# The second layer norm of an encoder layer: scale and shift on the turned tiles, GpSimd makes x2, tiles at multiples of 64 bytes

## The chip, the cores and the metric

The kernel runs on one core of a Trainium2 chip. The engines are named as the profile names them: PE is TensorE (matmuls and transposes), DVE VectorE, ACT ScalarE, POOL GpSimd, SP SyncE, whose queue issues most of the DMAs. The metric is the device time of one launch in microseconds (us), the median of the runs. On-chip memory is SBUF, with 128 partitions; matmul results land in PSUM.

## The reference

One layer of an encoder on a sequence of 1024 tokens, model width 1024, all in float32:

```python
x = layer_norm(DEEPNORM_ALPHA * x + 0.5 * swiglu_ffn(x, ffn1_w_gu[l], ffn1_w_down[l]), ln1_g[l], ln1_b[l])
x = layer_norm(DEEPNORM_ALPHA * x + hybrid_mixer(x, w_in[l], w_gla_a2[l], b_gla_a[l], gla_norm_g[l], w_out[l]),
               ln2_g[l], ln2_b[l])
x = layer_norm(DEEPNORM_ALPHA * x + 0.5 * swiglu_ffn(x, ffn2_w_gu[l], ffn2_w_down[l]), ln3_g[l], ln3_b[l])
```

The layer norm takes mean and variance over the 1024 features of a token and returns (x - mean) * rsqrt(var + 1e-5) * g + b. The feed-forward part is (silu(h @ w_g) * (h @ w_u)) @ w_down with an inner width of 2816. The mixer is one input projection, four heads of chunked gated linear attention, eight heads of sparse attention over selected keys, and one output projection, w_out. The case is about the line in the middle: the output projection, the second layer norm, and the first matrix products of the second feed-forward part, which read its result, x2. x2 is needed twice: as that part's input, and later, token by token, as the residual of the third layer norm.

## The kernel before, in words

Matrix products are done in three passes with a hi and a lo part: ACT rounds a float32 tile to its hi part (`Weights.split`, L96), DVE subtracts to get the lo part (L97), and PE sums hi by hi, lo by hi and hi by lo. Both operands are split so, weights and activations. The feed-forward products run on block sums of the matrices, a Strassen-like scheme with seven products instead of eight: of a quarter of the weights (tiles `rw`, sums made by POOL in L341 to L344, hi and lo parts `whiq` and `wloq`) and of the activations (quarters 11, 12, 21, 22 and their sums T1 to T4).

The tokens are eight blocks of 128. In the second layer norm's stage, at the end of `run`, the loop over the blocks b does the following for each:

- `proj_tok`: 24 matmuls give the second half (512 features) of the output projection in PSUM (`pt`). The first half was made before: of blocks 0 to 3 during the attention (L1645 stores it), of blocks 4 to 7 in a loop after it (tile `x1h`, L1669). The block's tile `acc[b]`, 128 tokens by 1024 features, was loaded with it; the profile calls it `x`.
- L1686, DVE: ALPHA times x plus the projection.
- `layer_norm` (L238 to L255): two `bn_stats` of 512 features, `bn_aggr`, variance plus epsilon (`ve`) on DVE; the reciprocal root `rs` by a power on POOL (L224, 128x1); `nb`, minus mean times rs, on DVE (L252); x * rs + nb on ACT, in place, 128x1024 (L253); times g on POOL (L254); plus b on DVE (L255). g and b are rows repeated in all partitions (`g_bc`, `b_bc`).
- L1688: 512 KB of x2 go to DRAM for the third norm's residual.
- From b = 2 on, `feed` turns block b - 2 in: `turn_in` makes, for each half, four PE transposes of 128x128 into one PSUM tile `tp` (two buffers, L282); ACT takes the hi part and DVE the lo part of it straight from PSUM, and ACT copies it back over the token-major half (L285, `keep`), because the sums T1 to T4 are made from turned halves later (L1270 to L1273: DVE, POOL, DVE, POOL; `split_turned` then splits them from SBUF). `b_h` and `b_l` are hi and lo parts of quarters 11 and 21; `xh` and `xl` those of the later quarters and sums.

Blocks 0 to 5 are turned inside the loop (4 and 5 as the last two); blocks 6 and 7 are turned in as fills between the matmuls of the first product of `gate_up`, together with the sums of block pairs (0,4), (1,5), (2,6), (3,7). That product is of quarters 11 and 21 with the gate weights; its two PSUM tiles are read by ACT's silu (L460), which loads its function table first, and are then used by the product after next.

The order: from the loop on, PE's instructions stand in the order in which the code makes them (`in_order`). The order on DVE, ACT, POOL and SP is set by a scheduler that plays the program through a timeline of its own when the kernel is built. At run time each engine takes its instructions strictly in the order so found and waits at each for what it needs. SBUF pools of the stage: `ln2` (`lp`, g, b and the `x1h` tiles), and `sums2` (`xp`).

Of the kernel before, what the change touches and what calls it, by code (L numbers as in the profile page):

```python
# [7 lines left out]
F32 = mybir.dt.float32  # L8
# [10 lines left out]
P = 128  # L19
# [96 lines left out]
class Block:  # L116
    def __init__(self, ctx, tc, aps):
# [9 lines left out]
        self.wpool = E(tc.tile_pool(name="wpool", bufs=1))  # L127
        self.ps_pj = E(tc.tile_pool(name="ps_pj", bufs=2, space=PSUM))
# [4 lines left out]
        nc.gpsimd.memset(self.neghalf, -0.5)  # L133
        self.w = Weights(tc, self.wpool)
# [5 lines left out]
        self.q_tiles = {}  # L140

# [88 lines left out]

    def layer_norm(self, t, g_bc, b_bc, scale=1.0, st=None):

        nc = self.nc
        made = st is not None
        if not made:
            st = self.small.tile([P, 2, 6], F32, tag="st", name=self.uid("st"))
            for c in range(2):
                nc.vector.bn_stats(st[:, c, :], t[:, c * 512 : (c + 1) * 512])  # L238
# [6 lines left out]
        if made:  # L245
            nc.vector.scalar_tensor_tensor(t, t, mv[:, 0:1], g_bc, ALU.subtract, ALU.mult)
            for c in range(2):
                cs = slice(c * 512, (c + 1) * 512)
                nc.vector.scalar_tensor_tensor(t[:, cs], t[:, cs], rs, b_bc[:, cs], ALU.mult, ALU.add)
        else:  # L250
            nb = self.small.tile([P, 1], F32, tag="nb", name=self.uid("nb"))
            nc.vector.scalar_tensor_tensor(nb, mv[:, 0:1], -1.0, rs, ALU.mult, ALU.mult)  # L252
            nc.scalar.activation(t, t, AF.Identity, bias=nb, scale=rs)  # L253
            nc.gpsimd.tensor_mul(t, t, g_bc)  # L254
            nc.vector.tensor_add(t, t, b_bc)  # L255
# [22 lines left out]
    def turn_in(self, src, j, name, keep=False):  # L278

        pt = self.ps_tp.tile([P, 4, P], F32, tag="tp", name=self.uid("tp"))  # L280
        for k in range(4):
            self.nc.tensor.transpose(pt[:, k, :], src[:, k * P : (k + 1) * P], self.ident)  # L282
# [13 lines left out]
    def feed(self, b, t):  # L296

        names = ("12", "22") if b >= NB // 2 else ("11", "21")
        for i, name in enumerate(names):
            self.turn_in(t[:, i * 512 : i * 512 + 512], b % 4, name, keep=True)  # L300
# [199 lines left out]
    def down(self, w_down, h_dram, t_dram, ps, load, after_block, after_all=None, ordered=None):  # L500
# [43 lines left out]
        def stat(b, c):  # L544
            if b not in stats:
# [1221 lines left out]
```

## Time and profile before

| | before |
|---|---|
| median of 3 runs | 1992.12 us (1988.24 to 1994.79) |
| profiled execution | 1986.98 us, its span 1985.2 us |
| granted PE clock, mean | 0.99 |
| busy: PE / DVE / ACT / POOL | 1932.2 / 1493.5 / 834.0 / 602.3 us |
| PE idle in the whole span | 53 us |
| stage of the change on the time axis | 1285 to 1365 us |
| PE waiting in that stage | 5.6 us, once |

A line of a timeline is: start, duration, engine, line of the kernel, operation, out<-in, shape, and in brackets how long the engine idled before it and what released it. A line of a chain of waits is: start, length, engine, tile and line. A line of the groups has the count, total busy time, mean duration in ns, and idle time with its releaser. Lines by tile have the shortest, the median and the longest duration in ns. A line of a table of stretches has the window, its length, busy time (and count) of PE, PE's weight loads, DVE, ACT and POOL, then granted clock, share of DMA time, GB/s.

### The profile page before, as it was taken

What the parts mean: (1) busy time and instruction counts of PE and PEld (TensorE: products, weight loads), DVE (VectorE), ACT (ScalarE), POOL (GpSimd) and SP (SyncE); (2) the same over time, 40 slices, a digit from 0 to 9 for tenths busy, and PEclk for the clock granted to TensorE, in tenths of its full rate; (3) what the DMA queues carried; (4) which work ended last, traced back from release to release, by engine and by line L of the source; (5) the groups of instructions that cost most, each with busy time, mean ns of one, the idle gap of its engine ahead of it and who ended that gap; (6) DMA issues with size and microseconds to landing.
All of it is one profiled execution on the core that took longest, in us unless ns stands there. A gap on an engine that the chain in (4) does not pass through costs nothing.

```text
span 1985.2 us, 26633 instructions
## 1 busy us (share of the span) xinstructions
PE 1932.2 (97%) x9576; PEld 1586.4 (80%) x9576; DVE 1493.5 (75%) x2333; ACT 834.0 (42%) x1340; POOL 602.3 (30%) x507
## 2 busy tenths in 40 slices
PE   9999999999999999999899899998999999999997
PEld 7788888888888788777687678787888888888886
DVE  8777887785677768899968567477778777857677
ACT  5333333334334345798553456354333233235331
POOL 4454454430001102144343000054444544510011
PEclk9999999999999999998999999999999999999999
DMA  5454454478656322022105741522444544587564
GB/s 180 146 185 152 155 182 146 149 254 305 200 175 202 99 85 85 22 65 62 45 33 170 186 106 39 201 97 95 159 138 147 187 148 149 178 290 251 193 199 151
DMA packets 193925, 298.43 MB, mean 150 GB/s; under 512 B 16496, under 2 KB 100608, under 8 KB 193792
## 3 DMA queue, kind: packets, MB, share of 16 engines
q1 hardware_dynamic: 189888, 291.48, 44.8%
q10 hardware_dynamic: 3264, 3.15, 0.5%
q0 software_dynamic: 640, 2.10, 0.3%
q8 instruction: 75, 1.23, 0.3%
q14 instruction: 58, 0.48, 0.1%
HBM read 205.96 MB, written 90.70 MB: 149 GB/s over the span
## 4 chain that ended last, share of the span: by engine, by line
PE 72%; DVE 13%; DMA 5%; issue 3%; ACT 3%; POOL 2%; SPq 0%; POOLq 0%; DVEq 0%; ACTq 0%
PE pd L536 18%; PE pq L362 11%; PE pq L363 11%; PE pq L364 11%; DVE junk L830 3%; PE pf L701 2%; PE pf L700 2%; PE pf L702 2%; PE pt L717 2%; PE pt L719 2%; PE pt L718 2%; PE pv L1186 2%; PE tpe L1170 2%; PE lg L1143 1%; DMA rd<-h_dram 1%
## 5 line engine op out<-in xcount | busy, mean ns | idle before, releaser
L97 DVE TENSOR_TENSOR wloq<-rw,whiq 128x512 fp32r<-128x512 f32 (+2 forms) x211 | 209.8, 996 | 130.3 <-ACT whiq L96 129.5
L97 DVE TENSOR_TENSOR wlod<-rd,whid 128x1024 fp32r<-128x1024 f32 x154 | 186.1, 1221 | 129.4 <-ACT whid L96 128.7
L96 ACT ACTIVATE whid<-rd 128x1024 fp32r<-128x1024 f32 x154 | 161.1, 1059 | 243.7 <-PE pd L536 167.5
L96 ACT ACTIVATE whiq<-rw 128x512 fp32r<-128x512 f32 (+2 forms) x211 | 164.2, 797 | 206.9 <-POOL rw L344 105.0
L536 PE MATMUL pd<-wlod,whid 128*128 128x512 f32 x616 | 239.8, 390 | 0.9 <-DVE wlod L97 0.8
L536 PE MATMUL pd<-whid,wlod 128*128 128x512 f32 x616 | 239.3, 389 | 0.0
L536 PE MATMUL pd<-whid 128*128 128x512 f32 x616 | 235.0, 391 | 0.7 <-ACT whid L96 0.7
L362 PE MATMUL pq<-b_h,whiq 128*128 128x512 f32 x576 | 226.1, 392 | 2.3 <-DVE c L411 1.3
L364 PE MATMUL pq<-b_h,wloq 128*128 128x512 f32 x576 | 224.9, 391 | 0.5 <-DVE wloq L97 0.5
L363 PE MATMUL pq<-b_l,whiq 128*128 128x512 f32 x576 | 225.0, 391 | 0.0
L224 POOL TENSOR_TENSOR rs<-ve,neghalf 128x1 f32<-128x1 f32 x24 | 35.4, 1476 | 540.5 <-DVE ve L242 540.5
L476 ACT ACTIVATE c<-c 128x512 f32<-128x512 f32 x80 | 50.7, 634 | 266.5 <-DVE c L398 169.7
L362 PE MATMUL pq<-xh,whiq 128*128 128x512 f32 x352 | 136.9, 389 | 0.0
L363 PE MATMUL pq<-xl,whiq 128*128 128x512 f32 x352 | 136.9, 389 | 0.0
L364 PE MATMUL pq<-xh,wloq 128*128 128x512 f32 x352 | 136.9, 389 | 0.0
L536 PEld LDWEIGHTS pd<-wlod,whid 128*128 128x128 f32 x616 | 115.7, 188 | 25.8 <-DVE wlod L97 2.1
L536 PEld LDWEIGHTS pd<-whid 128*128 128x128 f32 x616 | 115.5, 188 | 25.2 <-ACT whid L96 1.7
L536 PEld LDWEIGHTS pd<-whid,wlod 128*128 128x128 f32 x616 | 115.6, 188 | 24.1
L717 PE MATMUL pt<-whi,xh 128*128 128x512 f32 x320 | 131.3, 410 | 2.4 <-ACT stage L1531 1.6
L362 PEld LDWEIGHTS pq<-b_h,whiq 128*128 128x128 f32 x576 | 108.7, 189 | 25.8 <-ACT whiq L96 1.8
L364 PEld LDWEIGHTS pq<-b_h,wloq 128*128 128x128 f32 x576 | 108.6, 188 | 23.9 <-DVE wloq L97 1.1
L718 PE MATMUL pt<-wlo,xh 128*128 128x512 f32 x320 | 127.6, 399 | 0.0
(275 smaller groups left out, 4484.7 us busy)
## 6 DMA issues: line engine op xcount, KB each, us to landing
rw<-in_ffn_w_gu_dram SPq DMA_DIRECT2D x87, 512.0 KB, 4.3
rd<-h_dram SPq DMA_DIRECT2D x154, 256.0 KB, 3.5
h_dram<-c SPq DMA_DIRECT2D x148, 256.0 KB, 3.2
rt<-in_ffn_w_down_dram SPq DMA_DIRECT2D x44, 512.0 KB, 3.6
t_dram<-rt SPq DMA_DIRECT2D x44, 512.0 KB, 3.0
rd<-t_dram SPq DMA_DIRECT2D x88, 256.0 KB, 3.7
rd<-in_ffn_w_down_dram SPq DMA_DIRECT2D x66, 256.0 KB, 4.1
raw<-in_w_in_dram SPq DMA_DIRECT2D x20, 512.0 KB, 3.9
```

The lines of the kernel that those rows point to most:

```text
L96: self.nc.scalar.activation(hi, src, AF.Copy)
L97: self.nc.vector.tensor_sub(lo, src, hi)
L362: mm(bank, wh[:, k, :], xh[:, k, :], start=start, stop=False)
L363: mm(bank, wh[:, k, :], xl[:, k, :], start=False, stop=False)
L364: mm(bank, wl[:, k, :], xh[:, k, :], start=False, stop=stop)
L476: nc.scalar.activation(t, t, AF.Silu)
L536: nc.tensor.matmul(bank, left, right, start=(i == 0 and n == 0), stop=(i == ng - 1 and n == 2))
L700: nc.tensor.matmul(pt[:m], wh[:, k, :m], xh[:, k, :], start=(k == 0), stop=False)
L701: nc.tensor.matmul(pt[:m], wh[:, k, :m], xl[:, k, :], start=False, stop=False)
L717: nc.tensor.matmul(pt, xh[:, k, cols], wh[:, k % 2, :], start=(k == 0), stop=False)
L718: nc.tensor.matmul(pt, xh[:, k, cols], wl[:, k % 2, :], start=False, stop=False)
L830: V.tensor_scalar(junk[:, :n], scores[b], thr, None, ALU.is_ge, ALU.add, accum_out=cnt)
```

## The change

1. `normalize` takes the place of `layer_norm` in this stage: it ends with one DVE operation, (x - mean) * rs, 128x1024 in place. nb, the ACT pass, and the two passes for g and b on the token-major tile are gone from the way to the transposes.
2. After the transposes a feature lies in one partition, so g and b are columns: `ln2_gb` holds them as 128 x 2 x 8, loaded by two DMAs that pick single elements. `turn_in` makes four ACT operations of 128x128 from PSUM, with scale and bias by column, that write the turned half, and then splits that half from SBUF (`split_turned`): the lo difference now reads two SBUF operands.
3. x2 for the residual is made by POOL alone: for each half of a block a product with the g row (L1702) and a sum with the b row (L1703), into a tile of its own with two buffers, and a store of 256 KB (L1704).
4. The statistics of each block's first half are taken when that half is made, in the attention (blocks 0 to 3) and in the `x1h` loop (4 to 7), and kept in `stats`.
5. Small unused tiles (`edge`, `pad`), two widened ones (`one`, `heads`) and two that change places (`gn`, `ba`) move many SBUF tiles from addresses that are 32 beyond a multiple of 64 bytes to multiples of 64: among them the raw weight tiles in part, the accumulators, and tiles of the attention.

The arithmetic of the result is the same up to rounding. The diff, cut to its core; lines of the kernel after stand 5 to 16 further down than before:

```diff
@@ the constants
+        edge = E(tc.tile_pool(name="edge", bufs=1, side="right"))
+        edge.tile([P, 32], U8, name="edge")
...
+        self.const.tile([P, 32], U8, name="pad")
...
+        self.stats = self.const.tile([P, NB, 2, 6], F32, name="stats")
@@ layer norm
+    def normalize(self, t, st):
+        nc = self.nc
+        mv = self.small.tile([P, 2], F32, tag="mv", name=self.uid("mv"))
+        nc.vector.bn_aggr(mv, st)
+        ve = self.small.tile([P, 1], F32, tag="ve", name=self.uid("ve"))
+        nc.vector.tensor_scalar(ve, mv[:, 1:2], LN_EPS, None, ALU.add)
+        rs = self.small.tile([P, 1], F32, tag="rs", name=self.uid("rs"))
+        self.rsqrt(rs, ve, 1)
+        nc.vector.tensor_scalar(t, t, mv[:, 0:1], rs, ALU.subtract, ALU.mult)
...
-            nb = self.small.tile([P, 1], F32, tag="nb", name=self.uid("nb"))
-            nc.vector.scalar_tensor_tensor(nb, mv[:, 0:1], -1.0, rs, ALU.mult, ALU.mult)
-            nc.scalar.activation(t, t, AF.Identity, bias=nb, scale=rs)
-            nc.gpsimd.tensor_mul(t, t, g_bc)
-            nc.vector.tensor_add(t, t, b_bc)
@@ turn_in
-        self.w.split([t[:, :, j * P : (j + 1) * P] for t in self.sums[name]], pt)
-        if keep:
-            self.nc.scalar.activation(src.rearrange("p (k t) -> p k t", k=4), pt, AF.Copy)
+        g, b = self.affine
+        for k in range(4):
+            r = 4 * (int(name[0]) - 1) + k
+            self.nc.scalar.activation(
+                src[:, k * P : (k + 1) * P], pt[:, k, :], AF.Identity, bias=b[:, r : r + 1], scale=g[:, r : r + 1]
+            )
+        self.split_turned(src, j, name)
@@ run: in the attention, and the same line in the x1h loop
+                        nc.vector.bn_stats(self.stats[:, b - 1, 0, :], xh)
@@ run: loads
+            gb = xp.tile([P, 2, KD], F32, name="ln2_gb")
+            self.affine = [gb[:, i, :] for i in range(2)]
+            for t, v in zip("gb", self.affine):
+                nc.sync.dma_start(v, a[f"ln2_{t}"][0].rearrange("(k p) -> p k", p=P))
+            rows = [self.bcast_row(lp, a[f"ln2_{t}"], f"{t}_bc") for t in "gb"]
@@ run: the loop of the second norm
-                self.layer_norm(acc[b], g_bc, b_bc)
-                nc.sync.dma_start(x2_dram[b * P : (b + 1) * P, :], acc[b])
+                nc.vector.bn_stats(self.stats[:, b, 1, :], acc[b][:, 512:])
+                self.normalize(acc[b], self.stats[:, b])
+                for c in range(2):
+                    cs = slice(c * 512, (c + 1) * 512)
+                    x2 = lp.tile([P, 512], F32, tag="xh", name=self.uid("x2h"), bufs=2)
+                    nc.gpsimd.tensor_mul(x2, acc[b][:, cs], rows[0][:, cs])
+                    nc.gpsimd.tensor_add(x2, x2, rows[1][:, cs])
+                    nc.sync.dma_start(x2_dram[b * P : (b + 1) * P, cs], x2)
```

PE's instructions stand in the same order as before. On the other engines the scheduler found another order. Three places matter.

POOL at the end of the stage. `x_7` is the tile of block 7, `rs_11956` before and `rs_12000` after its reciprocal root. Before:

```order
L224 TENSOR_TENSOR rs_11899<-ve_11897,neghalf 128x1
L1271 TENSOR_TENSOR x_4_11509<-x_4_11509 128x512
L254 TENSOR_TENSOR x_6_11511<-x_6_11511,g_bc_11324 128x1024
L1273 TENSOR_TENSOR x_0_11502<-x_0_11502,x_4_11509 128x512
...
L344 TENSOR_TENSOR rw_12286<-rw_12286,rw_12284 128x4x128
L224 TENSOR_TENSOR rs_11956<-ve_11954,neghalf 128x1
L1273 TENSOR_TENSOR x_1_11503<-x_1_11503,x_5_11510 128x512
L254 TENSOR_TENSOR x_7_11512<-x_7_11512,g_bc_11324 128x1024
L1271 TENSOR_TENSOR x_6_11511<-x_6_11511 128x512
```

After:

```order
L1276 TENSOR_TENSOR x_5_11519<-x_5_11519 128x512
L350 TENSOR_TENSOR rw_12349<-rw_12351,rw_12349 128x4x128
L228 TENSOR_TENSOR rs_12000<-ve_11998,neghalf 128x1
L1278 TENSOR_TENSOR x_1_11512<-x_1_11512,x_5_11519 128x512
L351 TENSOR_TENSOR rw_12351<-rw_12351,rw_12349 128x4x128
L1702 TENSOR_TENSOR x2h_12003<-x_7_11521,g_bc_11329 128x512
L1702 TENSOR_TENSOR x2h_12007<-x_7_11521,g_bc_11329 128x512
L1703 TENSOR_TENSOR x2h_12003<-x2h_12003,b_bc_11331 128x512
L1703 TENSOR_TENSOR x2h_12007<-x2h_12007,b_bc_11331 128x512
L1276 TENSOR_TENSOR x_6_11520<-x_6_11520 128x512
```

Between the first rs of the stage and block 7's there are now 34 POOL operations of 128x512 (and six more rs), and block 7's four x2 operations stand ahead of the residual sum of block 6 (L1271 before, L1276 after).

ACT at the first silu of the second feed-forward part. Before:

```order
L253 ACTIVATE x_7_11512<-x_7_11512,nb_11958,rs_11956 128x1024
L96 ACTIVATE xh_11734<-tp_12081 128x4x128
L285 ACTIVATE x_6_11511<-tp_12081 128x512
L96 ACTIVATE xh_11734<-tp_12095 128x4x128
L460 ACT_TABLE_LOAD
L460 ACTIVATE c_12058<-pq_11994 128x512
L460 ACTIVATE c_12060<-pq_11995 128x512
L285 ACTIVATE x_6_11511<-tp_12095 128x512
L96 ACTIVATE xh_11734<-tp_12112 128x4x128
L285 ACTIVATE x_7_11512<-tp_12112 128x512
L96 ACTIVATE xh_11981<-x_6_11511 128x4x128
```

After:

```order
L289 ACTIVATE x_7_11521<-tp_12171,ln_gb 128x128
L289 ACTIVATE x_7_11521<-tp_12171,ln_gb 128x128 x3
L96 ACTIVATE xh_12034<-x_6_11520 128x4x128
L467 ACT_TABLE_LOAD
L467 ACTIVATE c_12111<-pq_12047 128x512
L467 ACTIVATE c_12113<-pq_12048 128x512
L96 ACTIVATE xh_11753<-x_7_11521 128x4x128
```

The hi part of block 6's residual, `L96 xh<-x_6`, which reads what POOL's L1271 (L1276 after) wrote, stood behind the silu and now stands ahead of it. The two `pq` tiles that silu reads are the ones the product after next writes into. That product's hi part of block 7 (`xh_11753<-x_7`, read from SBUF) stands behind the silu.

DVE around block 7's normalisation. Before, L255 of block 7 follows one lo difference from PSUM; after:

```order
L1277 TENSOR_TENSOR x_5_11519<-x_5_11519,x_1_11512 128x512
L97 TENSOR_TENSOR xl_12035<-x_5_11519,xh_12034 128x4x128 x2
L244 TENSOR_SCALAR x_7_11521<-x_7_11521,mv_11996,rs_12000 128x1024
L1275 TENSOR_TENSOR x_2_11513<-x_6_11520,x_2_11513 128x512
L97 TENSOR_TENSOR xl_11754<-x_6_11520,xh_11753 128x4x128 x2
L1277 TENSOR_TENSOR x_6_11520<-x_6_11520,x_2_11513 128x512
```

The normalisation of block 7 (L244) stands behind the sum L1277 of block 5 and two lo differences, and ahead of the lo differences of block 6, which now read SBUF.

More of the change, by code (lines that the diff above doesn't have):

```diff
@@ L244, in layer_norm @@
         self.rsqrt(rs, ve, 1)
[L245 to L250, printed above, removed]
-            nb = self.small.tile([P, 1], F32, tag="nb", name=self.uid("nb"))
-            nc.vector.scalar_tensor_tensor(nb, mv[:, 0:1], -1.0, rs, ALU.mult, ALU.mult)
-            nc.scalar.activation(t, t, AF.Identity, bias=nb, scale=rs)
-            nc.gpsimd.tensor_mul(t, t, g_bc)
-            nc.vector.tensor_add(t, t, b_bc)
+        nc.vector.scalar_tensor_tensor(t, t, mv[:, 0:1], g_bc, ALU.subtract, ALU.mult)
+        for c in range(2):
+            cs = slice(c * 512, (c + 1) * 512)
+            nc.vector.scalar_tensor_tensor(t[:, cs], t[:, cs], rs, b_bc[:, cs], ALU.mult, ALU.add)
     DOWN = (("A11", "11"), ("S2", "T2"), ("A12", "21"), ("S4", "22"), ("S1", "T1"), ("S3", "T3"), ("A22", "T4"))
@@ L299, in feed @@
         for i, name in enumerate(names):
[L300 removed]
+            self.turn_in(t[:, i * 512 : i * 512 + 512], b % 4, name)
     def quad_raw(self, w_gu, c0, halves=(0, 1), between=None):
@@ L544, in stat @@
         def stat(b, c):
-            if b not in stats:
-                stats[b] = self.small.tile([P, 2, 6], F32, tag="stats", name=self.uid("st"), bufs=NB)
             V.bn_stats(stats[b][:, c, :], acc[b][:, c * 512 : (c + 1) * 512])
@@ L592, in down @@
         turns = [(b, k) for b in range(4) for k in (0, 4)] if after_all else []
-        stats = {}
+        stats = [self.stats[:, b] for b in range(NB)]
         rest = []
@@ L1282, in item @@
                     else:
-                        self.turn_in(t(*src[name]), j, name, keep=True)
+                        self.turn_in(t(*src[name]), j, name)
                     if (j, name) == (3, "T4"):
@@ L1405, in run @@
             bias = {b: bp.tile([P, (b + 1) * P], BF16, name=f"bias{b}") for b in range(TOPK // P)}
-            one = bp.tile([P, 1], F16, name="one")
+            one = bp.tile([P, 32], F16, name="one")[:, :1]
             nc.gpsimd.memset(one, 1.0)
@@ L1485, in run @@
                 kz = [gp.tile([P, HT], F32, name=f"kz{j}") for j in range(2)]
-                heads = gp.tile([P, 2], F32, name="heads")
+                heads = gp.tile([P, 16], F32, name="heads")[:, :2]
                 nc.gpsimd.memset(heads, 0.0)
@@ L1653, in run @@
             lp = ln_stack.enter_context(tc.tile_pool(name="ln2", bufs=1, reuse_waits="tile"))
-            g_bc = self.bcast_row(lp, a["ln2_g"], "g_bc")
-            b_bc = self.bcast_row(lp, a["ln2_b"], "b_bc")
+            gb = xp.tile([P, 2, KD], F32, name="ln2_gb")
[3 more added lines that the diff above has]
+            rows = [self.bcast_row(lp, a[f"ln2_{t}"], f"{t}_bc") for t in "gb"]
             c1 = self.new_half(0)
@@ L1686, in run @@
                 nc.vector.scalar_tensor_tensor(acc[b][:, 512:], acc[b][:, 512:], ALPHA, pt, ALU.mult, ALU.add)
-                self.layer_norm(acc[b], g_bc, b_bc)
-                nc.sync.dma_start(x2_dram[b * P : (b + 1) * P, :], acc[b])
+                nc.vector.bn_stats(self.stats[:, b, 1, :], acc[b][:, 512:])
+                self.normalize(acc[b], self.stats[:, b])
+                for c in range(2):
+                    cs = slice(c * 512, (c + 1) * 512)
+                    x2 = lp.tile([P, 512], F32, tag="xh", name=self.uid("x2h"), bufs=2)
+                    nc.gpsimd.tensor_mul(x2, acc[b][:, cs], rows[0][:, cs])
+                    nc.gpsimd.tensor_add(x2, x2, rows[1][:, cs])
+                    nc.sync.dma_start(x2_dram[b * P : (b + 1) * P, cs], x2)
                 if b == 3:
```

10 lines of the change are left out of this document (3 added, 7 removed).

## The prediction

> **What bounds the kernel now.** I read the page's busy shares first, then the list of what TensorE (PE) waited for, then the chain of waits around the second layer norm.
>
> ```profile
> PE 1932.2 (97%) x9576; PEld 1586.4 (80%) x9576; DVE 1493.5 (75%) x2333; ACT 834.0 (42%) x1340; POOL 602.3 (30%) x507
> ...
> PE tp L282 <- DVE x L255: 5.6, 1, 5.6
> ```
>
> PE is busy 97% of a span of 1985.2 us, so it idles 53 us in all. What the other engines do counts only where PE waits for them. In the changed stage that is one wait of 5.6 us (total, times, longest). Up to then the chain goes through PE, with eight transposes in each block, 0.11 us each, and 6.35 us from block to block:
>
> ```profile
> 1296.26 0.87 PE tp L282 x8
> 1302.61 0.87 PE tp L282 x8
> ```
>
> PE's timeline shows the wait, and what it costs besides; the last line is from the table of stretches:
>
> ```profile
> 1347.13 0.39 PE L364 MATMUL pq<-b_h,wloq 128*128 128x512 f32 x1
> 1353.14 1.08 PE L282 MATMUL tp<-ident,x 128*128 128x128 f32 x4 [5.62 <-DVE x L255]
> ...
> 1356.58 0.63 PE L362 MATMUL pq<-b_h,whiq 128*128 128x512 f32 x1
> 1357.01 0.63 PE L363 MATMUL pq<-b_l,whiq 128*128 128x512 f32 x1
> ...
> 1360.07 0.39 PE L364 MATMUL pq<-b_h,wloq 128*128 128x512 f32 x1
> 1360.30 0.39 PE L362 MATMUL pq<-xh,whiq 128*128 128x512 f32 x1
> ...
> 1350.00:1360.00 10.00, 6.86 (x25) 5.67 (x26) 7.40 (x10) 6.94 (x12) 4.67 (x3) 0.66 0.13 52
> ```
>
> After the wait the starts are 0.43 us apart instead of 0.23, and the granted clock of that slice (last but two) is 0.66. From 1353.14 to 1360.30 PE runs 18 matmuls and 8 transposes: 18 x 0.23 plus 8 x 0.11 is 5.0 us at full clock, but it took 7.16, so the wait costs another 2.2. The stage can give back at most 5.6 + 2.2 = 7.8 us, and only if nothing else becomes late. The chain that led there:
>
> ```profile
> 1343.83 1.29 POOL rw L344
> 1345.12 0.96 POOL rs L224
> 1346.08 1.34 POOL x L1273
> 1347.42 1.93 issue
> 1349.39 2.35 POOL x L254
> 1351.77 1.24 DVE x L255
> 1353.14 1.08 PE tp L282 x4
> ```
>
> Block 7's reciprocal root (rs) stands on GpSimd (POOL) behind weight sums and residual sums; then follow ScalarE's (ACT) normalisation, POOL's g product and VectorE's (DVE) b sum. POOL's own timeline at both ends of the stage:
>
> ```profile
> 1287.41 0.57 POOL L224 TENSOR_TENSOR rs<-ve,neghalf 128x1 f32<-128x1 f32 x1 [118.70 <-DVE ve L242]
> ...
> 1329.81 2.65 POOL L254 TENSOR_TENSOR x<-x,g_bc 128x1024 f32<-128x1024 f32 x1 [1.37 <-ACT x L253]
> ...
> 1338.96 2.16 POOL L343 TENSOR_TENSOR rw<-rw,rw 128x512 f32<-128x512 f32 x1
> ...
> 1345.08 1.00 POOL L224 TENSOR_TENSOR rs<-ve,neghalf 128x1 f32<-128x1 f32 x1
> ```
>
> **The change, part one: when does block 7's rs come?** Before, POOL has one long product a block. Afterwards it has two products and two sums of 128x512, and the order of its instructions puts 7 rs and 34 operations of 128x512 (14 L1702, 14 L1703, two L1276, one L1278, three weight sums) ahead of block 7's rs. Their prices:
>
> ```profile
> L341 POOL TENSOR_TENSOR rw<-rw,rw 128x512 f32<-128x512 f32 x40 | 61.1, 1527 | 194.5 <-DVE wloq L97 194.5
> L342 POOL TENSOR_TENSOR rw<-rw x40: 1290/1616/1628, 42.5 to 1732.8; 128x512 f32<-128x512 f32 x40
> L1273 POOL TENSOR_TENSOR x<-x,x 128x512 f32<-128x512 f32 x4 | 6.1, 1519 | 2.2 <-DVE x L1272 2.2
> L224 POOL TENSOR_TENSOR rs<-ve,neghalf 128x1 f32<-128x1 f32 x8 | 7.0, 869 | 126.3 <-DVE ve L242 126.3
> ```
>
> The same operation takes 1.29 us at best (the middle one, min/median/max) and 1.5 in the mean of the others. Why it stretches shows in DVE's rows at the same moments:
>
> ```profile
> 1330.11 2.89 DVE L1272 TENSOR_TENSOR x<-x,x 128x512 f32<-128x512 f32 x1
> 1332.93 0.68 DVE L1686 SCALAR_TENSOR_TENSOR x<-x,pt 128x512 f32<-128x512 f32 x1
> ...
> 1337.85 2.12 DVE L255 TENSOR_TENSOR x<-x,b_bc 128x1024 f32<-128x1024 f32 x1
> ```
>
> L1272, two operands in SBUF, needs 0.6 to 0.7 alone (as L1686, which reads one operand from PSUM), but takes 2.89 while POOL's L254 runs from 1329.81 to 1332.46. L255 (1.24 in the chain above) takes 2.12, and then POOL's L343 2.16. So each makes the other wait. Bounds for the 34 operations: 34 x 1.29 = 43.9 and 34 x 1.62 (L342's median) = 55.1. The new stage has on DVE, for each block, one 128x1024 normalisation and two lo differences that now read the turned tile and its hi part from SBUF, where before the differences read PSUM; such work is beside POOL nearly always, so I take the means, 1.5: 51.0 us. Seven rs at 0.87 are 6.1. POOL also waits after each rs for DVE's normalisation before its first product: about 1 us in blocks 0 to 2, less in 3 to 6 where a sum of the block before fills the gap, together 4 (between 2 and 8). And L1276 and L348 wait for DVE's operands once or twice, 1 us. The stage starts at 1287.4 as before, and 1287.4 + 51.0 + 6.1 + 4 + 1 = 1349.5 for the start of rs of block 7, 1350.5 for its end, against 1346.1 now. A load of 7.9 us a block (4 x 1.5, 0.87, 1) against 6.35 us between PE's blocks says the same: POOL goes from ahead to behind.
>
> The Trainium skill, page "SBUF — State Buffer", section "Who interferes with whom", speaks against the change more strongly: VectorE with two SBUF inputs, or in its double-port mode, and GpSimd share one port pair as an exclusive lock for a whole instruction. The trace agrees (L1272's 2.89 us against 0.68); by the rule, some 25 DVE instructions of 0.6 us would go on top of 43.9 + 4.0, and rs would come at 1350.3 even without the other waits, where the rows give 1344.5 without them.
>
> **Part two: from rs to PE.** What goes: ACT's L253, nb, POOL's L254 and the b sum, 5 us of chain. What comes is one tensor_scalar of 128x1024. The trace has none of this form; the nearest reads and writes as much:
>
> ```profile
> L883 DVE TENSOR_SCALAR keep<-score,search 128x1024 f32<-128x1024 f32 x1 | 0.9, 936 | 0.0
> ```
>
> So 0.94 alone; beside POOL, which has L1278 and a weight sum just behind rs, 1.9 (as L255's 2.12). On DVE it stands behind L1277 of block 5 and two lo differences; these wait for L1276, two places ahead of rs on POOL (it ends near 1348.1), and with one hi part between them take to 1353. The normalisation ends near 1355, and PE's transposes start at 1355.2: a first wait of 7.7 us, 2.1 longer than now (ends: none at 1347.5, and 13).
>
> **Part three: what is late next.** Behind rs, POOL's order has block 7's four x2 operations ahead of L1276 of block 6. On ACT the hi part of that residual (L96) stands ahead of the silu of the first FFN product, whose PSUM banks PE's next product needs. Now:
>
> ```profile
> 1349.22 0.57 ACT L96 ACTIVATE xh<-tp 128x512 fp32r<-128x512 f32 x1
> ...
> 1351.65 1.28 ACT L460 ACT_TABLE_LOAD   x1
> 1352.95 1.09 ACT L460 ACTIVATE c<-pq 128x512 f32<-128x512 f32 x2
> ...
> 1356.57 0.62 ACT L96 ACTIVATE xh<-x 128x512 fp32r<-128x512 f32 x1
> ```
>
> Today table and silu run inside PE's wait and that hi part comes after them, at 1356.57. After: from 1355.1 five POOL operations at 1.6 (three beside DVE work) are 8.0, to 1363.1; then hi part 0.62, table 1.28, two silu 1.09, hi part of block 7 0.6: 1366.7. That is when the product that starts at 1360.30 now can start: **+6.4 us**. PE itself would have been ready at 1355.2 + 7.16 = 1362.4, so this second wait is 4.3 us; the price of the first wait is inside it. Whether the clock falls again after 4.3 us no row shows: 0 to 2.2, I take 1.1. The Trainium skill, "TensorE: Matmul & The Clock Gate", Part 1, has about 3.4 us idle as enough; by it the whole 2.2 is lost, 1.1 more than I count.
>
> **Part four: the rest.** Eight statistics of half a block move ahead of the stage, into attention and the x1h loop.
>
> ```profile
> L238 DVE BATCH_NORM_STATS2 st<-x 128x6 f32<-128x512 f32 x13 | 9.0, 689 | 0.2
> DMA to landing us min/median/max: 4.6/4.6/4.6
> L1173 ACT ACTIVATE et<-tpe 128x128 f32<-128x128 f32 x8 | 2.2, 272 | 6.0 <-PE tpe L1170 5.9
> 1210.00:1253.00 43.00, 40.85 (x412) 34.55 (x413) 29.30 (x62) 25.89 (x45) 0.00 (x0) 1.00 0.00 1
> ```
>
> In that stretch DVE is busy 29.3 of 43 us: four of 0.69 fit, 0 to 2.8 us, I take 0.5. The two loads of g and b as columns move 1,024 elements each; the like load of 256 (tile ba, second line) took 4.6 us, so up to some 18 us each. They lie in this stretch, where the DMA share is 0.00, 35 us before their first use: nothing. Without that cover they would hold the wide loads behind them by as much. The x2 stores halve; a stalled one holds two weight loads behind it on SyncE's queue, for weights whose first sums come a product later: nothing. ACT scales and shifts eight 128x128 pieces a block (0.27 each by L1173, 2.2 us of 6.35) in place of L253 and two copies: nothing.
>
> The new 64-byte multiples: the weight sums and kz lay at an odd multiple of 32 bytes in part, gg and gn at multiples of 64.
>
> ```profile
> L1523 POOL TENSOR_TENSOR gg<-gg,gn x4: 1284/1290/1484, 864.0 to 867.9; 128x512 f32<-128x512 f32 x4
> L1019 POOL TENSOR_TENSOR kz<-gk,gq x4: 1295/1298/1592, 845.3 to 1024.5; 128x512 f32<-128x512 f32 x4
> ```
>
> 1290 against 1298 ns: nothing that PE would see; 0, with 2 us either way.
>
> **Sum.** 6.4 + 1.1 + 0.5 = 8.0 us. The profiled execution took 1986.98 (1.8 around its span), 5.1 below the median of 1992.12; the difference added to either gives 1995 and **2000.1**. I say 2000.
>
> **Rivals.**
> (A) *POOL is not disturbed.* 34 x 1.29 + 7 x 0.57 + 4 ends rs at 1340; the normalisation is done by 1341, block 7's five POOL operations by 1347.6, before PE arrives. Both waits vanish: -7.8 + 0.5, 1985. For it: L342's 1290 and rs at 0.57; against it: the mean of 1.5. 9 in 100.
> (B) *The backlog just eats the gain.* At 1.4 an operation and 3 us of waits, rs ends at 1345, normalisation and differences at 1349, the five operations at 1356.5, silu and hi part at 1360.1: PE restarts where it does now, one wait in another place, clock loss as before. 0 to +2, 1993. 24 in 100.
> (C) *The shared resource costs in full*, as in the 2.89 of L1272: 1.62 an operation and 1.9 for each normalisation, POOL waiting 8: rs ends at 1358; all behind it moves 6 us more, +14, 2006. It decides from 1.55 us an operation on. 13 in 100.
> (D) *The multiples of 64 bytes do matter*, in ACT, DVE or DMA all over the program. PE's waits outside this stage, 47 us, are what could shrink: 1985 if an eighth does. The two rows above speak against it. 4 in 100.
> The forecast has 50 in 100.
>
> **How the numbers follow.** A measurement here can tell 0.3%, 6 us, from no change. The forecast's own range is 1995 to 2004: three parts in four of it lie over 6 us. Slower: 0.75 x 0.50 + 0.13 and a little of B, 0.52. Same: nearly all of B and a quarter of the forecast, 0.35. Faster: A and D, 0.13. The range goes from 1986 (A's time) to 2007 (C's).
>
> **What would show it.** Right: POOL's rs of block 7 near 1350 and POOL busy over 8 of 10 us from 1290 to 1350; PE with two waits, one at the transposes of block 7 (7 to 8 us) and one at the next product, for ACT (4 us); L1702 and L1703 at 1.5 us in the mean. Wrong in step one: rs before 1347. Wrong in step three: no wait at the product that reads xh. Wrong in all: L97's wlod off its 1221 ns.

## The result and the profile after

The changed kernel takes 2004.3 us in the median (2001.62 to 2005.75) against 1992.12 (1988.24 to 1994.79): a ratio of 1.0067, 95% interval 1.0052 to 1.0081. It is slower, by 12 us or 0.7%. The profiled execution took 2001.62 us with a span of 1999.9, 14.6 us above that of before (1986.98). Granted clock over the whole run: 0.987, before 0.990.

The page's first part and the list of what PE waited for from the stage on, after the change (engine, line, releaser: us in total, times, longest):

```profile
PE 1940.2 (97%) x9576; PEld 1590.0 (80%) x9576; DVE 1502.6 (75%) x2325; ACT 837.4 (42%) x1380; POOL 624.7 (31%) x531
```

```profile
PE tp L285 <- DVE x L244: 7.3, 1, 7.3
PE pq L369 <- ACT xh L96: 3.1, 1, 3.1
PE pd L543 <- ACT whid L96: 1.0, 1, 1.0
PE pq L370 <- DVE xl L97: 0.2, 1, 0.2
```

Where one wait of 5.6 us stood, there are two: 7.3 us at block 7's transposes and 3.1 us at the next product. But PE's waits account only for part of the loss: PE is also *busy* for 8 us more (1940.2 against 1932.2) with the same 9576 matmuls. Its timeline around the stage's end:

```profile
1356.57 1.09 PE L285 MATMUL tp<-ident,x 128*128 128x128 f32 x4 [7.31 <-DVE x L244]
...
1364.18 0.39 PE L371 MATMUL pq<-b_h,wloq 128*128 128x512 f32 x1
1367.65 0.50 PE L369 MATMUL pq<-xh,whiq 128*128 128x512 f32 x1 [3.08 <-ACT xh L96]
1368.37 0.50 PE L370 MATMUL pq<-xl,whiq 128*128 128x512 f32 x1 [0.22 <-DVE xl L97]
...
1371.18 0.63 PE L369 MATMUL pq<-xh,whiq 128*128 128x512 f32 x1
1371.61 0.63 PE L370 MATMUL pq<-xl,whiq 128*128 128x512 f32 x1
...
1372.82 0.40 PE L370 MATMUL pq<-xl,whiq 128*128 128x512 f32 x1
```

The product that reads xh started at 1360.30 before; now at 1367.65. After the second wait the starts of the matmuls are again 0.43 us apart for some 3.3 us. POOL at both ends of the stage shows the delay being built:

```profile
1289.13 0.57 POOL L228 TENSOR_TENSOR rs<-ve,neghalf 128x1 f32<-128x1 f32 x1 [118.82 <-DMA rw<-in_ffn_w_gu_dram]
...
1351.90 0.99 POOL L228 TENSOR_TENSOR rs<-ve,neghalf 128x1 f32<-128x1 f32 x1
...
1356.51 3.34 POOL L1702 TENSOR_TENSOR x2h<-x,g_bc 128x512 f32<-128x512 f32 x2 [0.63 <-DVE x L244]
1359.81 2.95 POOL L1703 TENSOR_TENSOR x2h<-x2h,b_bc 128x512 f32<-128x512 f32 x2
1362.72 1.29 POOL L1276 TENSOR_TENSOR x<-x 128x512 f32<-128x512 f32 x1
```

Block 7's rs starts 62.8 us after block 0's, where it was 57.7 before. And the four x2 operations of block 7 stand between its normalisation and L1276 of block 6. The second wait's chain goes exactly through them, behind L244 (start, duration, what):

```profile
1349.07 1.65 POOL x L1276
...
1350.74 1.75 DVE x L1277
...
1352.51 0.64 ACT xh L96
...
1353.18 1.57 DVE xl L97
1354.75 1.69 DVE x L244
...
1356.51 3.34 POOL x2h L1702 x2
...
1361.49 1.27 POOL x2h L1703
1362.76 1.26 POOL x L1276
...
1365.99 1.08 ACT c L467 x2
1367.08 0.53 ACT xh L96
```

Ahead of L244 block 7's rs is not on this chain. It ended at 1352.89, some 1.8 us before L244 started: on DVE, L244 stands behind two lo differences, and these wait, through L1277 and a hi part on ACT, for POOL's L1276 of block 5, two places ahead of rs. That L1276 had itself waited 1.2 us for DVE's lo differences. So POOL and DVE are both late here, and which of the two set the first wait is not shown.

**Where the time went.** I add up the starts of the same matmuls in PE's two timelines. Up to the stage, after is 1.7 us later; that is less than two executions of one kernel differ by, and I give it no cause. From the stage's first matmul to the 200th behind the restart of the xh product: 125.9 us before, 134.0 after, +8.1. From there to the end of the second gate and up products: 357.0 and 361.0, **+4.0**. The second down product: 210.8 and 211.1. Together 8.1 + 4.0 is 12.1 us, and the medians differ by 12.2.

The 4.0 was not in the prediction at all, and no wait shows it. It is seen in the table of stretches, in which the number of matmuls stands in brackets behind PE's busy time, with the granted clock, the DMA share and GB/s at the end. Before, and then after:

```profile
1600.00:1700.00 100.00, 100.00 (x443) 82.81 (x442) 78.69 (x83) 28.86 (x44) 51.70 (x34) 1.00 0.47 163
```

```profile
1600.00:1700.00 100.00, 100.00 (x438) 81.91 (x438) 76.29 (x87) 32.00 (x50) 43.39 (x29) 1.00 0.44 149
```

PE is busy without a break at a granted clock of 1.00 in both, and still does 438 matmuls where it did 443: from start to start it is 229.2 ns in the mean of this length instead of 226.7. (100 us divided by the count comes out about 1 ns low, since the count takes in the matmuls that reach over the window's two ends.) "Busy 100%" is thus no sign that the pace is the same; the count in brackets is.

### The profile page after: what moved, and what is told of

Read it like the earlier page. It is cut to its first block, busy times and chain, and to the rows that moved or that the text cites. A ratio compares the mean times of both kernels' runs of the same rounds, so it can differ in the third digit from the quotient of the medians.

```text
span 1999.9 us, 26702 instructions
## 1 busy us (share of the span) xinstructions
PE 1940.2 (97%) x9576; PEld 1590.0 (80%) x9576; DVE 1502.6 (75%) x2325; ACT 837.4 (42%) x1380; POOL 624.7 (31%) x531
## 4 chain that ended last, share of the span: by engine, by line
PE 68%; DVE 13%; DMA 7%; issue 4%; POOL 4%; ACT 4%; SPq 0%; POOLq 0%; DVEq 0%; ACTq 0%
PE pd L543 17%; PE pq L369 11%; PE pq L371 11%; PE pq L370 11%; DVE junk L835 3%; PE pf L705 2%; PE pf L706 2%; PE pf L707 2%; PE pv L1191 2%; PE tpe L1175 2%; DMA rd<-in_ffn_w_down_dram 1%; PE pt L722 1%; PE pt L724 1%; PE pt L723 1%; DMA t_dram<-rt 1%
## 5 line engine op out<-in xcount | busy, mean ns | idle before, releaser
L97 DVE TENSOR_TENSOR wloq<-rw,whiq 128x512 fp32r<-128x512 f32 (+2 forms) x211 | 213.6, 1014 | 132.1 <-ACT whiq L96 131.3
L97 DVE TENSOR_TENSOR wlod<-rd,whid 128x1024 fp32r<-128x1024 f32 x154 | 186.3, 1221 | 130.5 <-ACT whid L96 130.1
L96 ACT ACTIVATE whid<-rd 128x1024 fp32r<-128x1024 f32 x154 | 161.0, 1059 | 243.9 <-PE pd L543 167.3
L96 ACT ACTIVATE whiq<-rw 128x512 fp32r<-128x512 f32 (+2 forms) x211 | 163.8, 797 | 221.5 <-POOL rw L351 107.5
L370 PEld LDWEIGHTS pq<-b_l,whiq 128*128 128x128 f32 x576 | 109.4, 190 | 23.1
```

Source lines behind the costliest of these rows:

```text
L96: self.nc.scalar.activation(hi, src, AF.Copy)
L97: self.nc.vector.tensor_sub(lo, src, hi)
L370: mm(bank, wh[:, k, :], xl[:, k, :], start=False, stop=False)
```

## The experiments

Three theories stood against each other. *Chain*: the loss lies in the stage, where POOL's four x2 operations a block make rs late and then hold L1276 (the prediction's account). *Padding*: the new multiples of 64 bytes of the small tiles cost time by themselves. *Neighbour*: the new 64-byte tile ln2_gb moves the tiles behind it. Among them are b2 and t1, the tiles that PE streams against the weights (the moving operands) in the second gate and up products, and this slows PE's pace. All ratios are against the kernel before on the same chip; "stage", "gate and up" and "down" are the three lengths above (before: 125.9, 357.0, 210.8), each from one profiled execution, so a sum of them can miss a median by some 3 us.

**The paddings alone.** On the kernel before:

```diff
+        edge = E(tc.tile_pool(name="edge", bufs=1, side="right"))
+        edge.tile([P, 32], U8, name="edge")
-        one = bp.tile([P, 1], F16, name="one")
+        one = bp.tile([P, 32], F16, name="one")[:, :1]
...
-                heads = gp.tile([P, 2], F32, name="heads")
+                heads = gp.tile([P, 16], F32, name="heads")[:, :2]
```

> The kernel before with the address padding alone (the small tile at the right edge, the two widened tiles, gn and ba exchanged), which puts the accumulators and tiles of the attention at multiples of 64 bytes; the second layer norm is unchanged. Theory: multiples of 64 bytes do nothing, so the time is that of the kernel before, 1992 +- 3 us, with the wait of 5.6 us before block 7's transposes. Rival: the addresses matter over the whole program; then it is 4 us or more away from 1992, either way, and ACT, DVE or DMA durations differ.

Measured: 1989.11 us against 1990.11, 0.9996 [0.9985, 1.0007]; the wait at the transposes stays at 5.6 us and PE does 442 to 443 matmuls in 100 us. *Padding* falls for these tiles: rounded to 64 bytes, they neither gain nor lose. The run leaves out the change's unused tile `pad`, and as built it leaves the weights, b2 and t1 where they were; in the next run the weights have moved.

**ln2_gb at 512 bytes.** The changed kernel with the tile of g and b widened, so that b2 and t1 begin at the same remainder modulo 256 as the weights again:

```diff
-            gb = xp.tile([P, 2, KD], F32, name="ln2_gb")
+            gb = xp.tile([P, 128], F32, name="ln2_gb")[:, : 2 * KD].rearrange("p (i k) -> p i k", i=2)
```

> The changed kernel with one difference: the tile of g and b as columns takes 512 bytes of a partition instead of 64, so that the activation tiles behind it (b2, t1) lie at the same address modulo 512 as the weight tiles and the xh tiles again. In the changed kernel's second feed-forward part matmuls start 229 ns apart, in the kernel before 227. Theory: the 64 bytes moved b2 and t1 out of step with the weights; so the spacing is 227 ns again, the granted clock's and the waits' part stays, and the time is 4.4 us less than the changed kernel's, about 2000. Rival: the slower pace comes from the restart after the waits or from the run; then the spacing stays at 229 and the time at 2004.

Measured: 1999.09 against 1990.11, 1.0042 [1.003, 1.0054]. Gate and up is back at 357.0 us, and the table of stretches has the old count:

```profile
1600.00:1700.00 100.00, 100.00 (x443) 82.84 (x442) 77.23 (x86) 32.53 (x50) 46.78 (x32) 1.00 0.44 147
```

The stage keeps its loss (134.2 us, waits of 7.2 and 4.6 us). So the two losses are separate, and the tile's size alone makes the one of 4 us. As built, the weights begin 384 bytes lower here than in the kernel before, `pad` and `stats` included, and that costs nothing in this length.

**64 unused bytes in the kernel before.** The other way round, with none of the change's work:

```diff
+            xp.tile([P, 16], F32, name="gap")
```

> The kernel before with an unused tile of 64 bytes ahead of b2 and t1 of the second feed-forward part, and nothing else. Theory of the address step: matmuls of that part start 229 ns apart instead of 227, 390 us of it are 4.4 us longer: 1996 to 1997. Rival (the pace has to do with the changed layer norm): 1992, spacing 227.

Measured: 1994.21 against 1990.11, 1.0016 [1.0007, 1.0024]. Gate and up takes 361.0 us, as after the change, and the wait at the transposes is 5.5 us, as before it:

```profile
1600.00:1700.00 100.00, 100.00 (x438) 81.90 (x437) 80.04 (x86) 31.10 (x48) 47.43 (x32) 1.00 0.42 142
```

A tile that nothing reads or writes costs this length 4.0 us (the medians differ by 4.1, the interval of the ratio is 1.4 to 4.8 us). *Neighbour* is shown from both sides.

**128 and 256 unused bytes.** To see what the distance has to be, the same line with 32 and with 64 elements.

> The kernel before with an unused tile of 128 bytes ahead of b2 and t1 of the second feed-forward part. If what counts is the address modulo 128, the matmuls start 227 ns apart as before; if it is modulo 256 or 512, 229 ns, and the part is 4 us longer.

> The kernel before with an unused tile of 256 bytes ahead of b2 and t1 of the second feed-forward part (64 and 128 bytes made its matmuls start 229 ns apart or more). If the address modulo 256 counts, they start 227 ns apart again and the part is as long as before; if it is modulo 512, it stays 4 us longer.

Measured, one execution each: 1997.31 us with 128 bytes (before: 1989.73), 1990.62 with 256 (before, one execution: 1988.66). Gate and up takes 361.7 and 357.0 us. First 128, then 256:

```profile
1600.00:1700.00 100.00, 100.00 (x436) 81.66 (x436) 77.97 (x84) 29.95 (x46) 48.92 (x33) 1.00 0.42 142
```

```profile
1600.00:1700.00 100.00, 100.00 (x443) 82.84 (x442) 79.67 (x83) 28.60 (x43) 51.86 (x35) 1.00 0.45 154
```

In the kernel before, as built, the weights, xh, b2 and t1 all begin at the same remainder modulo 256. Moved by 64 or 128 bytes, b2 and t1 slow PE's pace; by 256 (here) or 512 (the wide ln2_gb) they don't. Of the distances tried, the multiples of 256 are free and the others are not. In the changed kernel the other tiles of the change moved weights, xh, b2 and t1 alike, and ln2_gb moved b2 and t1 by another 64: there too the distance to the weights is 64.

The address of b2 and t1 alone does not decide it. With 128 unused bytes and with the wide ln2_gb they begin at the same bytes of their partition (141760 and 186816), and the starts are 229.6 ns apart in the first and 226.7 in the second; the weights stand 384 bytes apart in the two. In every run the weights and xh moved together, so which of them the distance counts from is not told apart. PE's starts also show where the time goes. With 128 bytes, matmuls that read b2 or t1 start 233.0 and 232.6 ns apart, those that read xh 227.3; with 64 bytes it is 229.6, 230.3 and 228.8, the slow ones among xh being the 12 or so right behind b2 or t1; in the kernel before all three have 226.7. Other tiles stand behind the gap too, but the slow starts begin with the first matmul that reads b2 or t1.

**Block 7's x2 left out.** On the changed kernel, to price the second wait:

```diff
-                for c in range(2):
+                if b == NB - 1:
+                    nc.sync.dma_start(x2_dram[b * P : (b + 1) * P, :], rows[0])
+                for c in range(2 if b < NB - 1 else 0):
```

> The changed kernel without block 7's four x2 operations on GpSimd (the g row is stored in place of block 7's x2, so the residual of the last 128 tokens is wrong); everything ahead of block 7's rs on GpSimd stays in the same order. Theory: the second PE wait comes from those four operations, which hold up block 6's residual sum and with it ACT's silu; so the first wait stays at 7.3 us, the second vanishes with its loss of clock, and the time is 4 to 5 us less than the changed kernel's: 1999 to 2000. Rival (the second wait comes from the lo differences that read SBUF): it stays above 2 us, time 2002 to 2004.

The row of g is stored in its place. Measured: 1994.97 against 1989.85, 1.0026 [1.0016, 1.0036]; stage 128.7 us, 5.3 less than after the change. On PE's timeline one wait of the stage is left; the second fence has POOL's rows, the third one of ACT's:

```profile
1355.40 1.11 PE L285 MATMUL tp<-ident,x 128*128 128x128 f32 x4 [7.58 <-ACT x L289]
```

```profile
1350.30 0.99 POOL L228 TENSOR_TENSOR rs<-ve,neghalf 128x1 f32<-128x1 f32 x1
...
1357.47 1.28 POOL L1276 TENSOR_TENSOR x<-x 128x512 f32<-128x512 f32 x1 [3.19 <-ACT x L289]
```

```profile
1352.87 1.08 ACT L467 ACTIVATE c<-pq 128x512 f32<-128x512 f32 x2
```

rs is nearly as late as after the change, and L244 ends at 1354.84; the transposes then wait for ACT's L289, 7.6 us in all. The second wait is gone: L1276 of block 6 starts at 1357.47 instead of 1362.72, and the silu no longer stands behind it. The scheduler put the silu ahead of the hi part of block 6's residual here, so it ran at 1352.87 instead of 1365.99. The edit thus did two things, and the 5.3 us are the price of the four operations together with the ACT order in which the silu waits for what they hold up. The other 2.8 of the stage's 8.1 us are mostly the later first wait, with the clock behind it. That is *chain*, with the path of the first wait left open.

**The normalisation back on ACT.** The other edit of the stage, undone alone:

```diff
-        nc.vector.tensor_scalar(t, t, mv[:, 0:1], rs, ALU.subtract, ALU.mult)
+        nc.vector.scalar_tensor_tensor(ve, mv[:, 0:1], -1.0, rs, ALU.mult, ALU.mult)
+        nc.scalar.activation(t, t, AF.Identity, bias=ve, scale=rs)
```

> The changed kernel with the normalisation done by ACT again, as rs * x + nb (nb by one small DVE operation), in place of the DVE pass of 128x1024. GpSimd's operations stay, two weight and residual sums fewer stand ahead of block 7's rs. Theory (DVE and GpSimd hold each other up): without that DVE pass GpSimd's x2 products and sums fall from a mean of 1.47 us to 1.35 or less and rs of block 7 comes 3 to 6 us earlier than 1351.9; the first wait is 2 to 5 us. Rival (only the count of GpSimd's operations matters): their mean stays at 1.47, rs comes only the 2.9 us earlier that two operations fewer give, less the longer chain through ACT; the first wait stays at 6 to 8 us.

Measured: 1995.69 against 1989.85, 1.003 [1.0019, 1.0041]; stage 128.1 us. The first wait falls to 4.4 us and the second to 2.2. But POOL's operations did not get faster, by the groups of the stage (count | busy, mean ns of one | idle before):

```profile
L1704 POOL TENSOR_TENSOR x2h<-x2h,b_bc 128x512 f32<-128x512 f32 x16 | 24.6, 1559 | 0.1
L1703 POOL TENSOR_TENSOR x2h<-x,g_bc 128x512 f32<-128x512 f32 x16 | 22.2, 1402 | 6.3 <-DMA x_dram<-x2h 3.0 <-ACT x L245 1.6 <-DMA rw<-in_ffn_w_gu_dram 1.6
```

A mean of 1.48 us, as with the normalisation on DVE (1.47: 1499 and 1431 ns). So part of my account falls: DVE's tensor_scalar is not what stretches POOL's operations; DVE's differences and sums are left as the cause, and were not isolated. What ACT's version saves is mostly the count: rs of block 7 starts at 1345.25, 57.1 us behind block 0's instead of 62.8, since 31 operations of 128x512 stand ahead of it instead of 34, and three of 1.5 are 4.5 of those 5.6 us. POOL waits 1.6 us for the normalisations (5.1 after the change) but 3.0 for stores of x2h. That is the expectation's rival, which had only the count of operations matter, though the first wait fell as the theory had it.

**No x2 work in the stage.** On the kernel with the wide ln2_gb, the stage stores the normalised blocks as they are, and POOL scales and shifts them in the second down product, after they are read back:

```diff
+                rows = [self.bcast_row(pools["u"], a[f"ln2_{t}"], f"{t}2_bc") for t in "gb"] if n == 2 else []
+                ...
+                        (nc.gpsimd.tensor_add if i else nc.gpsimd.tensor_mul)(half, half, row[:, c * 512 : (c + 1) * 512])
...
-                for c in range(2):
-                    ...
+                nc.sync.dma_start(x2_dram[b * P : (b + 1) * P, :], acc[b])
```

> The changed kernel with the 512-byte tile, and GpSimd's scale and shift of x2 taken out of the second layer norm's stage: the normalised tile is stored, and g and b are applied by GpSimd after it is loaded again for the third layer norm, where GpSimd has little to do. Theory (GpSimd's backlog makes both waits): rs of block 7 comes before 1338 us, both PE waits of the stage vanish, 13 us less than the changed kernel from the waits and the pace of 4.4 on top: 1984 to 1987. Rival one (the waits come from the lo differences that now read SBUF, or from the single DVE pass): the waits stay above 4 us, 1996 or more. Rival two: GpSimd's work slows DVE in the last part by as much as it saves: PE waits there grow by 5 us, 1990.

Measured: 1993.12 against 1990.11, 1.0019 [1.001, 1.0028]. In the stage the waits all but vanish: rs of block 7 at 1340.95 (it was expected before 1338), no wait at the transposes, 0.9 us at the product; stage 119.3 us, 6.6 under before. DVE's groups there show the shared resource from its other side: the same instructions without POOL's x2 operations beside them. First this kernel (stage), then after:

```profile
L244 DVE TENSOR_SCALAR x<-x,mv,rs 128x1024 f32<-128x1024 f32 x8 | 7.5, 934 | 4.7 <-POOL rs L228 4.7
L97 DVE TENSOR_TENSOR b_l<-x,b_h 128x512 fp32r<-128x512 f32 x8 | 5.2, 688 | 2.1 <-ACT b_h L96 2.1
```

```profile
L244 DVE TENSOR_SCALAR x<-x,mv,rs 128x1024 f32<-128x1024 f32 x8 | 11.3, 1410 | 6.9 <-POOL rs L228 6.9
L97 DVE TENSOR_TENSOR b_l<-x,b_h 128x512 fp32r<-128x512 f32 x8 | 7.6, 979 | 4.2 <-ACT b_h L96 4.2
```

b_l, two operands in SBUF, takes 0.69 us in the mean without and 0.98 with them; the normalisation 0.93 and 1.41. The Trainium skill, "SBUF — State Buffer", section "Who interferes with whom", has tensor_tensor with both inputs in SBUF contend with GpSimd's reads, and names tensor_scalar among the operations that can take the port pair which VectorE shares with GpSimd; these rows agree. But the gain comes back as a loss in the down product, 223.2 us (+12.4). Its list of waits for PE:

```profile
PE pd L543 <- ACT whid L96: 4.3, 1, 4.3
PE pd L543 <- DVE wlod L97: 3.7, 3, 2.2
```

There POOL has 32 operations more and the queue two row loads of 512 KB more, ahead of the down weights. The chain of waits has both, a row load and then late x2 work (L1333), which leads to a sum on DVE at 1813.86:

```profile
1769.35 12.09 DMA g_bc<-in_ln_g_dram
...
1785.29 28.54 POOL acc L1333 x15
```

So the expectation's second rival came true: what the stage gains is lost later.

**The x2 work divided.** The same, but only for the last blocks: 6 and 7 (`range(6, NB)` in both places), and 5 to 7.

> The changed kernel with the 512-byte tile; GpSimd makes x2 in the stage for blocks 0 to 5 only, and for blocks 6 and 7 after they are loaded again for the third norm. Ahead of block 7's rs stand 29 GpSimd operations of 128x512 instead of 34, and none of x2 behind it. Theory (the backlog): rs of block 7 near 1345 us instead of 1352, its wait at the transposes 2 to 3 us instead of 7.2, no second wait; the late work is 8 operations instead of 32, which DVE's last part bears: 1988 to 1991, as the kernel before or a little under. Rival (the waits hang on the lo differences from SBUF): both waits stay, 1997 to 2000.

> As the split of x2 at block 6, but at block 5: 25 operations ahead of block 7's rs. Theory: rs of block 7 near 1341 us as in the kernel that makes all of x2 late, no wait at the transposes, 6 us under the kernel before from the stage; 12 late operations cost 1 to 3 us in the last part: 1985 to 1989. Rival (late work costs in proportion, 12 us for 32 operations): 4.5 us, 1990 to 1992.

Measured: from block 6 on, 1992.14 against 1989.85, 1.0011 [1.0001, 1.0021]; stage 123.7, down 217.9. From block 5 on, 1990.01 against 1989.85, 0.9997 [0.9987, 1.0007]; stage 120.7, down 216.9. rs of block 7 starts at 1346.99 and 1345.16, later than expected, and both times lie about 1 us above what was expected. Moving three blocks' work gives the stage 5.2 us, and the down product takes 6.1 back, although POOL has only 12 operations more there. PE's wait there, and the chain that leads to it, from block 5 on:

```profile
1791.93 2.07 PE L543 MATMUL pd<-whid 128*128 128x512 f32 x4 [4.20 <-ACT whid L96]
```

```profile
1771.98 9.17 DMA acc<-x_dram
1781.17 9.55 DMA rd<-in_ffn_w_down_dram
```

Before, the same reload of the blocks took 6.92 us from 1773.05 on and the down weights behind it 9.69. Here the chain names transfers, no POOL work: with the reload and the weights now run four row loads (two for x2, two for the last layer norm) where there were two. That they lengthen the reload is what the next kernels try.

**And the last layer norm's rows later.** Its two rows are needed only at the end, so they are loaded two products later; the x2 work is late from block 5 and from block 4 on:

```diff
+                elif m == 2 and self.later:
+                    self.later.pop()()
...
-                ln.extend(self.bcast_row(pools["ln"], a[f"{norm}_{t}"], f"{t}_bc") for t in ("g", "b"))
+                def last_rows():
+                    ln.extend(self.bcast_row(pools["ln"], a[f"{norm}_{t}"], f"{t}_bc") for t in ("g", "b"))
+
+                self.later = [last_rows]
```

> As the split of x2 at block 5 (g and b applied late for blocks 5 to 7), and the rows of g and b of the third layer norm are loaded two products later, so that no more is loaded at the start of the last part than in the kernel before. There the split kernel waited 4.2 us for weights behind the two added row loads. Theory: that wait goes, with the clock it costs; the stage keeps its 5 us: 1984 to 1987, below the kernel before by 0.2 to 0.3%. Rival (the late GpSimd work itself, by slowing DVE, is the cost): the wait or its like stays, 1989 to 1992.

> The same with the late part from block 4 on: four operations of GpSimd fewer in the stage (21 ahead of block 7's rs), four blocks late, 16 operations of 128x512. Theory: the stage as in the kernel that makes all of x2 late (6.6 us under the kernel before), 0 to 2 us lost in the last part to GpSimd beside DVE: 1983 to 1987. Rival: 16 late operations collide with DVE's splits and PE waits 3 us or more there: 1988 to 1991.

Measured: from block 5 on, 1985.68 against 1989.73, 0.9978 [0.9969, 0.9987]; from block 4 on, **1983.97 against 1989.73, 0.9974 [0.9962, 0.9985]**. Both beat the kernel before, by 0.2 to 0.3%, and the changed one. From block 5 on, PE's wait for the down weights falls from 4.2 to 2.3 us and does not vanish, and in the stage 2.0 us at the transposes are left. From block 4 on: rs of block 7 at 1340.38, stage 119.1 us, down 213.8, and what is left of PE's waits from the stage on is

```profile
PE pd L543 <- DVE wlod L97: 1.2, 1, 1.2
PE pd L543 <- ACT whid L96: 1.0, 1, 1.0
PE pq L370 <- DVE xl L97: 0.9, 1, 0.9
```

with the reload back to its old length:

```profile
1766.14 6.71 DMA acc<-x_dram
...
1772.87 9.89 DMA rd<-in_ffn_w_down_dram
```

So the change's idea holds once three things are put right: not more POOL work in the stage than POOL has room for, b2 and t1 at the weights' remainder again, and no extra loads ahead of the down weights. The sum of the two lengths (-6.8 and +3.0, -3.8) is somewhat less than the medians' 5.8, inside the error given above; the same sum for the version from block 5 on is near 0 against a measured 4.1, and its profiled execution was 3 us above its median.

## Why the prediction was right, and where not

Predicted 2000 us, slower; measured 2004.3, slower. The mechanism was the one forecast for the stage, and the total was too low by a term that was put at nothing. The measured time lies just above the forecast's own range (1995 to 2004). It is inside the wider one only because that reaches to the time of rival C, whose price of 1.62 us an operation did not come (1.49 in the mean, though its 8 us of waits did); that much is luck. Step by step; all times of after are taken 1.7 us earlier here, since its stage began that much later.

- *Part one, rs of block 7.* Predicted start 1349.5, measured 1351.90 - 1.7 = 1350.2. That it came so close is partly luck: POOL waited some 8.4 us on the way and not 5, and the seven rs took 4.8 us and not 6.1. POOL's operation was put at 1.5 us, and the groups of the stage agree:

```profile
L1702 POOL TENSOR_TENSOR x2h<-x,g_bc 128x512 f32<-128x512 f32 x16 | 23.8, 1499 | 6.1 <-DVE x L244 5.1 <-DMA rw<-in_ffn_w_gu_dram 1.1
L1703 POOL TENSOR_TENSOR x2h<-x2h,b_bc 128x512 f32<-128x512 f32 x16 | 22.8, 1431 | 0.3
L289 ACT ACTIVATE x<-tp,ln_gb 128x128 f32<-128x128 f32 x64 | 23.4, 465 | 26.2 <-PE tp L285 15.7 <-POOL x2h L1703 4.8 <-issue 4.8
```

  The reason was right only in part: with DVE's normalisation undone POOL's mean stayed at 1.48.
- *Part two, the first wait.* Predicted 7.7 us, measured 7.3, and by the path that the prediction names: not rs, but the lo differences behind L1276 of block 5 ended last ahead of L244 (1354.7 - 1.7 = 1353.0; predicted 1353). The normalisation took 1.76 us in the median and 0.80 at best, against 1.9 and 0.94 (instructions of this line after the change, min/median/max in ns):

```profile
L244 DVE TENSOR_SCALAR x<-x,mv,rs x8: 800/1760/1783, 1289.7 to 1354.7; 128x1024 f32<-128x1024 f32 x8
```

- *Part three, the second wait.* The restart was to come 6.4 us later; it came 7.35 - 1.7 = 5.6 later. The wait was to be 4.3 us and was 3.1 plus 0.2, since POOL's five operations took from 1356.51 to 1364.02, 7.5 us and not 8.0; ACT's steps behind them, from 1364.05 to 1367.60, took the 3.6 us they were put at. The clock loss behind it was taken at 1.1: from 1369.17 to 1372.82 PE started nine matmuls 0.41 us apart instead of 0.23, 1.6 us lost. The Trainium skill, "TensorE: Matmul & The Clock Gate", Part 1, has some 3.4 us of idle time as enough for half the clock; here half the clock (granted 0.50 from 1369.4 to 1372.6) followed a wait of 3.1 us, or 3.5 from start to start (1364.18 to 1367.65), so the trace does not contradict the page. 5.6 + 0.2 + 1.6 = 7.4, and the slower pace of the stage's last 200 matmuls adds some 0.3 (45.6 us with 64 unused bytes, 45.3 before): with the measured 8.1 that leaves 0.4, which the first two starts behind the wait hold (0.72 and 0.34 us apart).
- *Part four, statistics.* 0.5 us was taken; whatever it is lies inside the differences between executions ahead of the stage, and no run isolates it.
- *Part four, paddings.* Predicted 0, measured 0.9996 [0.9985, 1.0007]. Right, and so rival D, in which they pay, falls.
- *Part four, ln2_gb: the step that failed.* The prediction priced the loads of g and b as columns (at nothing, as they are) and looked at the multiples of 64 bytes of the small tiles, but did not ask where a new tile of 64 bytes puts the tiles behind it. b2 and t1 moved by 64 bytes against the weights, and the second gate and up products, which stream them, pay: +4.0 us. That this was "nothing that PE would see" was drawn from POOL rows (1290 against 1298 ns), and these say nothing of PE.
- *Part four, ACT.* The 128x128 pieces were put at 0.27 us from a row that reads PSUM in another stage; L289 took 465 ns in the mean. It lay beside other work, as foreseen.
- *Rivals.* B's backlog and C's full price bracketed what happened: rs ended at 1351.2, between B's 1345 and C's 1358. A, an undisturbed POOL, did not come: its operations took 1.47 us in the mean. The kernel without x2 work in the stage has rs where A had it (1340.95), but by fewer operations; the sums on POOL ahead of that rs still take 1.6 to 1.7 us.

The sum had 8.0 us; the stage lost 8.1, and the pace 4.0. The test "L97's wlod off its 1221 ns" held: 1221. What was missing from the list of tests was the count of matmuls in a stretch in which PE never waits.

## What to carry to other kernels

Before work is moved to an engine that feeds a chain, count what stands ahead of the chain's next instruction on that engine, and what stands *behind the last* one: here four operations behind the last normalisation, with a silu that had to wait for what they held up, made 5.3 of 8.1 us. Half of the same work a stage later, with other loads out of its way, made the kernel faster than before; all of it later did not. When a tile is added to a pool, look where the tiles behind it land. And compare the number of matmuls in a fixed stretch, not only busy shares and waits.

## What the runs showed of the hardware that I had not expected

- The pace of back-to-back matmuls of 128x128 on 128x512 (fp32r) depends on where the moving tiles begin relative to the weights (or to xh, which moved with them): in the gate and up length one starts every 226.7 ns when they have the weights' remainder modulo 256 bytes, every 229.2 when b2 and t1 are 64 bytes off, 229.6 at 128, 226.7 again at 256 and 512, at a granted clock of 1.00 in the stretch shown. In 357 us 64 bytes make 4 us, and no wait shows it. The same bytes for b2 and t1 are fast with one place of the weights and slow with another.
- A POOL operation of 128x512 costs 1.26 to 1.29 us at best and about 1.5 in the mean beside DVE; whether DVE or ACT normalises makes no difference to that mean (1.47 and 1.48).
- A wait of 3.1 us (3.5 from start to start) was followed by half the clock for 3.3 us.
